# A hybrid attention step: the decode sample as two instruction streams, the sparse keys in a stream of their own, and other margins in the planner's clock

## The chip, the cores and the metric

The kernel runs on one NeuronCore of a Trainium2 chip. The time is the device time of one execution in microseconds (us). Five engines matter: TensorE (PE, with its weight loads counted as PEld), VectorE (DVE), ScalarE (ACT), GpSimd (POOL) and SyncE (SP), which here only issues DMAs. Each works through its own instruction list in the order in which the program wrote it; they wait for each other through semaphores.

## The reference

One layer of an encoder on 2048 prompt frames (16 blocks of 128) and on a decode sample of 8 streams with 16 new frames each (one further block of 128 rows, number 16), which has a cache of 256 rows per stream. RMSNorm, one input projection to 5680 columns, three kinds of attention, a gated output projection with residual, and a final RMSNorm:

```
h = rmsnorm(x) @ w_in          # q, k, v, z of groups A, B, C; indexer iq, iw, ik; forget gate fa
A (8 heads):  causal softmax(q.k*s + c[t]-c[s]) v,  c = cumsum(log_sigmoid(fa + b_f))
B (8 heads, 2 kv heads):  score[t,s] = sum_h iw[t,h]*relu(iq[t,h].ik[s]);  keep the top 256 keys
              softmax(q.k*s + t5_bias[bucket(s-t)]) v  over the kept keys
C (8 heads):  softmax(q.k*s + c_rel[clip(s-t)]) v  over the own chunk of 64 and the 8 before
y = x + concat(oA, oB, oC) * silu(z) @ w_out;  rmsnorm(y)
```

The sample does the same against cache and new rows, with top 68 in B. Keys, values and gates are outputs as well.

## The kernel before, in words

**Arithmetic.** Each float32 operand is split into a high and a low float16 part, and a product is three matmuls. So a projection of 512 tokens by 128 columns is 8 x 3 = 24 matmuls of 512 columns, and each step of attention has a "low" part, Pl, which POOL or DVE subtracts out of the exponentials Pf.

**Streams and the planner.** The program's instructions are not written in a fixed order. Generator functions ("streams") each yield conditions and emit instructions, and `drive` (from line 436) chooses which stream takes its next step. It keeps a model of the engines, `Clock`: `Timed` (line 196 is its call into the engine, which is why the profile puts nearly all instructions on L196) gives each emitted instruction a planned cost, and `Clock.op` a planned end. A stream yields `need(tiles, ps=..., at=...)`, the planned time at which these tiles are ready and the PSUM banks free; or a `gate`, which is 0 or infinite; or `landed`, which waits until a projection group has been stored for 7 us. Conditions without a PSUM bank are "soft": the earliest of them is taken once it is within 200 ns (`AHEAD`) of PE's planned time. Otherwise the first of the other streams, in the order in which they were given, that is ready by PE's planned time takes its step. Streams further behind are so filler. Four services (`exp`, `low`, `evac`, `end`) hold follow-up jobs: exponential, low part, evacuation of a projection, end of a unit. All of this happens when the program is written: on the chip there are only the five lists that come out. PE, ACT, DVE and POOL keep the planned order.

**The work.** First norm and the indexer's projections. Then, in one run of `drive`:

- *Fill*: 21 projection groups, each with 256 weight columns over all 17 blocks (`load_stream`, `fill_stream`, `groups` from line 832). A group is "kv" (key and value columns, stored as outputs) or "qz" (query columns to `qTd`, gates to `szd`). They use the PSUM tag `pj` (two banks). `HO = 'ACCACCAA'` is the order of the eight pairs of dense heads; four qz groups and one kv group of B stand between them. `last[...]` says after which group four heads' projections are complete.
- *Dense units*: 16 heads, A and C in the order of `HO`, four units of 512 queries each (`DenseA`, `DenseC`). A head's keys and values are prepared by `prep_stream` (`K1`, `Ka`, `V` tiles) once its group has landed. The streams `maxima`, `rows`, `scores`, `products` work through the units; four steps of Pf and Pl are in flight (`PB = 4`). Results go to `gTd` (tile `gs`).
- *Indexer and selection*: `score_stream` (tiles `rl`, `acc`) and `select_stream` for blocks 2 to 15. Selection finds the top 256 by a search of ten iterations, in each of which ACT sums signs (`ssg`) and POOL steps the threshold on 128 x 1 tiles (`es`, `eg`, `iv`, `us`, `hv`); then DVE breaks ties, and the mask is stored to `negd`. The last instruction of a block writes `bad` on POOL.
- *Sample* (`sample_stream`, from line 1349): begins when all 14 selections are done, and works in tiles that the indexer and selection no longer use (`acc`, `yy`, `cum`, `eq`, `rl`, `qi`), cut into pieces: keys and query matrix, values, softmax, products. One stream takes the heads in turn: keys in five groups, scores, softmax (`smx`, `smb`), then the products of the head before (`srs`), then this head's values. 16 A and C heads, then its own selection (`select_s`), then 8 B heads. Every four heads are stored to `gTd` (`gs4`, which lies in `yy`).
- *Sparse units* (B, prompt): two per block, in the order 15 down to 0 (`ORDER`). `b_prep` prepares keys, values and biases (`KaB`, `K1B`, `VB`). It stands at the end of `prep_stream`, behind the last dense head's preparation, and waits until the fill has ended, since its tiles take the space of the projection's.
- *Output*: `out_all` opens when all dense units have ended and `b_prep` is through; a block's output projection (72 matmuls of 512 columns from tile `gac`) may begin some time after its sparse units, block 16 when the sample stream is over. It is the last of the fillers.

The streams' order before was: selection, weight loads, products, rows, indexer, scores, maxima, preparation, sample, and as fillers projection and output.

Of the kernel before, what the change touches and what calls it, by code (L numbers as in the profile page):

```python
# [162 lines left out]
class Stream:  # L163


    def __init__(self, steps, slack=SLACK):
        self.steps, self.wait, self.live, self.slack = steps, None, True, slack

    def soft(self):

# [2 lines left out]
    def at(self):  # L173
        if not callable(self.wait):
            return 0.0
        return self.wait() + (0.0 if self.soft() else self.slack)

    def step(self):
        try:
# [5 lines left out]
class Timed:  # L185
# [5 lines left out]
    def __getattr__(self, what):  # L191
# [3 lines left out]
        def call(*args, **kw):  # L195
# [10 lines left out]
            if e == "PE":  # L206
                cost = max(29.0, math.prod(ins[-1].shape[1:]) / 2.4 + 2.5)
                if ins[-1].dtype == F32:
                    cost *= 4
            elif e == "DVE":  # L210
                if what == "scalar_tensor_tensor":
                    cost = (129 if len(ins) > 2 else 68) + 1.042 * m
                elif what == "tensor_copy" and ins[0].dtype != F32:
                    cost = 68 + 0.26 * m if "ps" not in str(ins[0].tensor) else 68 + 0.52 * m
                elif what == "tensor_tensor_scan":
                    cost = 130 + 2.09 * m
                else:
                    cost = 68 + 1.042 * m + (70 if kw.get("accum_out") is not None else 0)
            elif e == "ACT":
                src = (ins or aps)[0]  # L220
                cost = 52 + 0.836 * m + (0 if clock.psum(src) else 40) + (92 if len(ins) > 1 or len(out) > 1 else 0)
                if clock.psum(src) and src.dtype == F16 and "Q" in out[0].tensor.name:
                    cost += 134
            elif e == "POOL":
                if what == "memset":
                    cost = 40 + 0.83 * m
                elif m <= 8:
                    cost = {1: 310, 2: 330, 3: 360}.get(len(ins), 360) if what == "tensor_scalar" else 270
                else:
# [35 lines left out]
def hybrid_step(ctx, tc, x_prompt, x_sample, cache_a_k, cache_a_v, cache_a_logf, cache_b_k, cache_b_v,  # L265
# [150 lines left out]

        return max(clock.slot((ps.key, t), 1 if t in ("tr", "o") else 2) for t in tags)

    def need(*tiles, ps=(), at=0.0):

        return Need(lambda: max(clock.at(*tiles), bank(*ps) if ps else 0.0, at), bool(ps))

    def gate(open_):

# [4 lines left out]
        return lambda: 0.0 if n <= 0 else marks[n - 1] + 7000.0 if len(marks) >= n else INF  # L429

    queues = {k: Queue() for k in ("exp", "low", "evac", "end")}
    services = [Stream(q.steps()) for q in queues.values()]
    for s in services:
        s.step()

# [398 lines left out]
    for k, ch in enumerate(HO):  # L834
        p = npair[ch]
        npair[ch] += 1
        if 2 <= k < 7:
            groups += [(group_b, max(k - 3, 0), int(k > 2))]
            last[2] = last[3] = len(groups)
        if k:  # L840
            groups += [(group_a if ch == "A" else group_c, p, w) for w in range(2)]
        heads += [(ch, 2 * p, len(groups)), (ch, 2 * p + 1, len(groups))]
        last[(0 if ch == "A" else 4) + p // 2] = len(groups)
    loaded, ngr, grouped = [], [0], []

    def load_stream():
# [153 lines left out]
    def scores(i, want_sum, sl, out):  # L1000
# [17 lines left out]
        for k0 in range(0, n, 512):  # L1018
            w = min(512, n - k0)
            for h in range(8):  # L1020
                yield need(qi, kiT, ps=("s1",))
                p = s1()
                mm(p[:, :w], qi[:, h, :], kiT[:, k0:k0 + w], start=True, stop=True)
                r = sl.tile([128, 512], F32, name="rl")
# [321 lines left out]
            G.memset(CN[0:64, 576:640], NEG)  # L1346


    def sample_stream():
        def big(nm, bufs, dt=F16):  # L1350
            return sl.tile([128, SEQ], F32, name=nm, bufs=bufs).bitcast(dt)

# [59 lines left out]
        def load(dst, src, g0, n):  # L1412
            for ap, j0, nj in src:
                a, b = max(j0, g0), min(j0 + nj, g0 + n)
                if a < b:
                    SP.dma_start(dst[:, a - g0:b - g0, :], ap[:, a - j0:b - j0, :])

        def ahead(nm, src):

            def one(g0):  # L1420
                n = min(4, 17 - g0)
                t = row(nm)
                load(t, src, g0, n)
                return t

            nxt = [one(0), one(4)]
            for g0 in range(0, 17, 4):
                yield g0, min(4, 17 - g0), nxt.pop(0)
                if g0 + 8 < 17:
                    nxt.append(one(g0 + 8))  # L1430

        def keys(src):
            Ka = KaS
# [169 lines left out]
            V.tensor_tensor(nsel, wk, acc, ALU.is_equal)  # L1603
            V.tensor_scalar(nsel, nsel, NEG, None, op0=ALU.mult)

        yield from gate_sums()
        yield landed(grouped, last[sorder[0]])
        after = None
        order = [4 * g + r for g in sorder + [2, 3] for r in range(4)] + [0]
        for k, hg in enumerate(order[:-1]):  # L1610
            g, r = divmod(hg, 4)
            if hg == 8:
                if after is not None:
                    yield from after()
                    after = None
                yield from select_s()
                yield landed(grouped, last[2])
            if r == 0:
                qp4 = sl.tile([128, 4, 128], F16, name="qp4", bufs=1)
                q24 = sl.tile([128, 4, 128], F16, name="q24", bufs=1)  # L1620
                rows = [qTd[e, g * 256:(g + 1) * 256, SEQ:NT].rearrange("(h d) t -> d h t", d=64) for e in range(2)]
                SP.dma_start(qp4[0:64], rows[0])
                SP.dma_start(qp4[64:128], rows[0])
                SP.dma_start(q24[0:64], rows[1])
            if hg < 8:
                ks, vs, bias = parts(cak, sak, hg), parts(cav, sav, hg), gate_bias(hg)
            elif hg >= 16:
                ks, vs, bias = parts(cck, sck, hg - 16), parts(ccv, scv, hg - 16), rel_bias(hg - 8)
            else:
                ks, vs, bias = parts(cbk, sbk, g - 2), parts(cbv, sbv, g - 2), rel_bias(hg - 8)  # L1630
            new = hg < 8 or hg >= 16 or r == 0
            more, bias = bias, next(bias)
            if new:
                Ka = yield from keys(ks)
            yield from more
            hl = yield from softmax(qp4[:, r, :], q24[0:64, r, :], Ka, bias)
            if after is not None:
                yield from after()
                yield landed(grouped, last[order[k + 1] // 4])
            if r == 0:  # L1640
                SP.dma_start(sz4, szd[g * 4:(g + 1) * 4, 4, :, 0:64].rearrange("h p d -> p h d"))
            if new:
                yield from values(vs)

            def after(hl=hl, sz=sz4[:, r, :], gs=gs4, r=r, g=g):
                yield from products(*hl, sz, gs[:, r, :])
                if r == 3:
                    for e in range(2):
                        SP.dma_start(gTd[e, g * 256:(g + 1) * 256, SEQ:NT].rearrange("(h d) t -> d h t", d=64),
                                     gs[e * 64:(e + 1) * 64])  # L1650
        yield from after()

    sorder = sorted([0, 1, 4, 5], key=lambda g: last[g])

# [241 lines left out]
    def run(units, may, others, fillers=()):  # L1896
# [41 lines left out]
                queues["end"].add(finished(u))  # L1938
                ndone[0] += 1

        drive(*others[:2], Stream(products()), Stream(rows()), *others[2:3], Stream(scores()), Stream(maxima(), 400.0), *others[3:], *fillers)

    def find_flag():

# [34 lines left out]
    def prep_stream():  # L1979
        for n, h in enumerate(heads):  # L1980
            yield gate(lambda: ndone[0] >= 4 * (n - 1) and (h.kind == "A" or tabled[0]))
            yield landed(grouped, h.after)
            yield from h.prep()
        yield gate(lambda: not fill_s.live)
        yield from b_prep()
        aw_done.append(1)

    aw_done = []

    def smp_stream():  # L1990
        yield gate(lambda: state["selected"] == 14)
        yield from sample_stream()

    def out_all():
        yield gate(lambda: len(ended) >= na and aw_done)
        aw_end.close()
        o = Out()
        closers.append(o.end)

        def open_(b):  # L2000
            if b == 16:
                return not smp_s.live
            n = na + 2 * (ORDER.index(b) + 1)
            return len(ended) >= n and (ended[n - 1] + 12000.0 < clock.t["PE"] or len(ended) == na + len(b_units))

# [2 lines left out]
    for u in units + b_units:  # L2008
        if isinstance(u, DenseA):
            u.open_ = u.head.open_  # L2010
    smp_s = Stream(smp_stream(), 300.0)
    run(units + b_units, lambda u: True, [Stream(select_stream(), 0.0), load_s, Stream(score_stream()), Stream(prep_stream(), 300.0),
                                          smp_s], [fill_s, Stream(out_all())])
    fv = flagged[0]
    closers.pop(1).close()
    sl_end.close()
# [82 lines left out]
```

## Time and profile before

| | |
|---|---|
| median of 3 runs | 2649.38 us (2643.98 to 2650.48) |
| profiled execution | 2649.79 us, span 2648.0 us |
| mean granted PE clock | 0.973 |
| busy share of the span | PE 91%, weight loads 63%, DVE 68%, ACT 52%, POOL 42% |
| instructions | 69046 |
| HBM | 160.37 MB read, 84.85 MB written, 93 GB/s over the span |

How to read it: the page cuts the span into 40 slices (66.2 us each) and gives each engine's busy share in tenths, with the clock that TensorE was granted below. A table by stage does the same for windows that one chooses. A tile's answer lists the instructions that write or read it, with the shortest, median and longest duration in ns and the start of the first and the last. The list of waits says who waited for whom, in us, how often, and the longest. Matmuls overlap: a run of matmuls has a busy time that is shorter than the sum of their durations.

### The profile page before, as it was taken

Reading aid. Unit: us, or ns where it says so; the run is one execution under the profiler, and the core shown is the slowest. Engines: PE = TensorE matmul, PEld = TensorE weight load, DVE = VectorE, ACT = ScalarE, POOL = GpSimd, SP = SyncE. Lnnn points to the kernel's source line nnn. Section 1 sums busy time; section 2 is a strip of 40 time slices with the busy share of each in tenths; the row PEclk is TensorE's granted clock in tenths of the full one; section 3 lists DMA queues with packets and bytes.
Section 4 is the critical chain, followed back from the end, with each engine's and each line's share of the span. In section 5 each row is a group of like instructions: output and inputs, shape, how many; then the busy total and the mean of one; then the engine's idle time right before and its main releaser. Section 6 shows DMA issues by size and latency. Waiting matters only on the chain. (4 is left out here: it accounts for less than half of the span.)

```text
span 2648.0 us, 69046 instructions
## 1 busy us (share of the span) xinstructions
PE 2397.8 (91%) x26752; PEld 1674.7 (63%) x26838; DVE 1802.8 (68%) x4900; ACT 1381.3 (52%) x2734; POOL 1100.3 (42%) x1730
## 2 busy tenths in 40 slices
PE   4998999999999998999999999478899999999995
PEld 3666677766766776686776876355455555555543
DVE  6333778876787868778685566487866677778542
ACT  6324666766656774766744454365554444444110
POOL 0012556663443544534452043255665444544100
PEclk9999999999999999999999999689999999999997
DMA  6247323434343222233445433643533334334531
GB/s 192 60 92 198 92 67 80 107 96 99 94 94 106 71 76 76 72 103 83 120 99 124 120 76 81 135 94 67 144 83 86 79 83 106 84 86 108 127 99 26
DMA packets 553189, 257.24 MB, mean 97 GB/s; under 512 B 376064, under 2 KB 541760, under 8 KB 552592
## 3 DMA queue, kind: packets, MB, share of 16 engines
q1 hardware_dynamic: 552848, 252.71, 38.8%
q8 instruction: 212, 3.47, 0.6%
q14 instruction: 129, 1.06, 0.1%
HBM read 160.37 MB, written 84.85 MB: 93 GB/s over the span
## 5 line engine op out<-in xcount | busy, mean ns | idle before, releaser
L196 POOL TENSOR_TENSOR Pl<-Pf 128x512 f16<-128x512 f32 (+3 forms) x688 | 683.4, 1003 | 582.2 <-ACT Pf L196 544.6
L196 PE MATMUL pj<-wt,hT 128*128 128x128 f16 (+1 forms) x8568 | 779.2, 243 | 11.3 <-DVE ev L196 10.9
L196 PEld LDWEIGHTS <-hT 128*128 128x128 f16 x8976 | 653.2, 98 | 117.5 <-issue 22.0
L196 ACT ACTIVATE Pf<-st,sh 128x512 f32<-128x512 f32 (+1 forms) x496 | 297.9, 613 | 282.9 <-DVE st L196 111.1
L196 PEld LDWEIGHTS <-Pf 128*128 128x128 bf16 x5472 | 314.9, 98 | 104.2 <-issue 9.8
L196 PE MATMUL pj<-wo,gac 128*128 128x512 f16 x1224 | 290.5, 383 | 13.2 <-DMA gac<-gTd 11.6
L196 PE MATMUL pj<-hT,wt 128*128 128x512 f16 (+1 forms) x1440 | 293.6, 348 | 0.3 <-DVE ev L196 0.3
L196 PEld LDWEIGHTS <-Pl 128*128 128x128 f16 x2736 | 255.3, 99 | 18.5 <-POOL Pl L196 16.4
L196 DVE SCALAR_TENSOR_TENSOR acc<-rl,iws,acc 128x512 f32<-128x512 f32 (+3 forms) x266 | 196.2, 738 | 87.1 <-ACT rl L196 82.5
L196 DVE CUSTOM_DVE_ANT_0 jk<-s,ng 128x512 bf16<-128x512 f32 (+3 forms) x304 | 188.7, 621 | 84.6 <-PE s L196 67.4
L196 ACT ACTIVATE Pf<-st,ncb 128x512 f32<-128x512 f32 (+1 forms) x320 | 192.1, 623 | 92.8 <-PE st L196 80.3
L196 DVE TENSOR_REDUCE mx<-s 128x1 f32<-128x512 f32 (+2 forms) x320 | 185.0, 603 | 67.0 <-PE s L196 66.1
L196 ACT ACTIVATE rl<-s 128x512 f32<-128x512 f32 (+3 forms) x304 | 161.3, 544 | 110.8 <-PE s L196 55.7
L196 ACT ACTIVATE ev<-pj 128x512 f32<-128x512 f32 (+4 forms) x211 | 115.2, 546 | 194.0 <-PE pj L196 181.3
L196 PE MATMUL o<-V,Pf 128*128 128x65 f16 x3296 | 213.2, 194 | 1.0 <-ACT Pf L196 0.9
L196 PE MATMUL o<-V,Pl 128*128 128x65 f16 x1648 | 196.2, 193 | 13.3 <-POOL Pl L196 12.3
L196 PEld LDWEIGHTS <-wt 128*128 128x128 f16 x1440 | 126.3, 98 | 129.2 <-issue 13.9
L196 PEld LDWEIGHTS <-gac 128*128 128x128 f16 x1224 | 116.5, 98 | 139.5 <-DMA gac<-gTd 12.7
L196 PE MATMUL st<-qp,Ka 128*128 128x512 f16 (+3 forms) x544 | 180.9, 335 | 8.8 <-ACT Pf L196 8.7
L196 ACT ACTIVATE eq<-acc,us 128x384 bf16<-128x384 f32 (+13 forms) x126 | 165.4, 1313 | 39.6 <-POOL us L196 38.0
L196 PE MATMUL st<-Q,K 98*128 98x512 f16 (+3 forms) x544 | 182.2, 336 | 1.7 <-ACT Q L196 1.7
L196 PE MATMUL o<-VB,Pf 128*128 128x65 f16 (+1 forms) x2176 | 132.4, 194 | 3.6 <-DVE rq_t L196 1.9
(449 smaller groups left out, 4299.8 us busy)
## 6 DMA issues: line engine op xcount, KB each, us to landing
wst<-in_w_in SPq DMA_DIRECT2D x84, 256.0 KB
gac<-gTd SPq DMA_DIRECT2D x34, 384.0 KB
out<-ev SPq DMA_DIRECT2D x96, 128.0 KB
qTd<-ev SPq DMA_DIRECT2D x96, 128.0 KB
szd<-ev SPq DMA_DIRECT2D x96, 128.0 KB
qp<-qTd SPq DMA_DIRECT2D x96, 128.0 KB
out<-xr SPq DMA_DIRECT2D x17, 512.0 KB
xt<-in_x_prompt SPq DMA_DIRECT2D x16, 512.0 KB
```

What stands on the lines that cost most here:

```text
L196: r = f(*args, **kw)
```

## The change

1. The sample becomes two streams. `first` does gate sums, the keys, scores and softmax of each head, and the selection; `second` loads and splits the values and does the products. `first` may be at most two heads' softmaxes ahead (`len(done) >= k - 1`), and each begins the loads of its next head (`begin`) at the end of the one in hand.
2. The streams' order becomes: selection, weight loads, sample first, sample second, products, rows, indexer, scores, maxima, preparation, sparse preparation, and the fillers as before.
3. `b_prep` becomes a stream of its own, gated by the end of the fill alone.
4. The fourth qz group of B moves from before the last two A pairs to the end of the fill; the sample's B heads and the sparse preparation then wait for the whole fill.
5. The planner's clock: a `late` margin for soft conditions (150 ns for the services, 400 for selection, 200 for the indexer), higher planned costs for POOL's `tensor_scalar` on up to 8 columns with two and three operands, and a `room` condition for the indexer's matmul: its output buffer `rl` must be due within 500 ns.

The core of the diff:

```
-        return self.wait() + (0.0 if self.soft() else self.slack)
+        return self.wait() + (self.late if self.soft() else self.slack)
...
-                    cost = {1: 310, 2: 330, 3: 360}.get(len(ins), 360) if what == "tensor_scalar" else 270
+                    cost = {1: 320, 2: 440, 3: 520}.get(len(ins), 520) if what == "tensor_scalar" else 270
...
-    def need(*tiles, ps=(), at=0.0):
-
-        return Need(lambda: max(clock.at(*tiles), bank(*ps) if ps else 0.0, at), bool(ps))
+    def need(*tiles, ps=(), at=0.0, room=None):
+
+        return Need(lambda: max(clock.at(*tiles), bank(*ps) if ps else 0.0, at,
+                                clock.slot((room[0].key, room[1]), room[0].bufs) - 500.0 if room else 0.0), bool(ps))
...
-    services = [Stream(q.steps()) for q in queues.values()]
+    services = [Stream(q.steps(), late=150.0) for q in queues.values()]
...
-        if 2 <= k < 7:
+        if 2 <= k < 6:
             groups += [(group_b, max(k - 3, 0), int(k > 2))]
-            last[2] = last[3] = len(groups)
...
         last[(0 if ch == "A" else 4) + p // 2] = len(groups)
+    groups += [(group_b, 3, 1)]
+    last[2] = last[3] = len(groups)
...
-                yield need(qi, kiT, ps=("s1",))
+                yield need(qi, kiT, ps=("s1",), room=(sl, "rl"))
...
+        def begin(nm, src):
+            early[nm] = [one(nm, src, 0), one(nm, src, 4)]
...
+        def first():
+
+            yield from gate_sums()
+            yield upto(order[0])
+            for k, hg in enumerate(order):
...
+                if fresh(hg):
+                    Ka = yield from keys(stored(hg)[0])
+                yield from more
+                yield gate(lambda: len(done) >= k - 1)
+                weights.append((yield from softmax(qp4[:, r, :], q24[0:64, r, :], Ka, bias)))
+                if k + 1 < len(order):
+                    yield upto(order[k + 1])
+                    if fresh(order[k + 1]) and order[k + 1] != 8:
+                        begin("kn", stored(order[k + 1])[0])
+
+        def second():
+
+            yield upto(order[0])
+            begin("vn", stored(order[0])[1])
+            for k, hg in enumerate(order):
+                g, r = divmod(hg, 4)
+                if fresh(hg):
+                    yield from values(stored(hg)[1])
...
+                if k + 1 < len(order) and fresh(order[k + 1]):
+                    yield upto(order[k + 1])
+                    begin("vn", stored(order[k + 1])[1])
+                yield gate(lambda: len(weights) > k)
+                yield from products(*weights[k], sz4[:, r, :], gs4[:, r, :])
+                done.append(k)
...
-        drive(*others[:2], Stream(products()), Stream(rows()), *others[2:3], Stream(scores()), Stream(maxima(), 400.0), *others[3:], *fillers)
+        drive(*others[:4], Stream(products()), Stream(rows()), *others[4:5], Stream(scores()), Stream(maxima(), 400.0), *others[5:], *fillers)
...
+    def sparse_prep_stream():
         yield gate(lambda: not fill_s.live)
         yield from b_prep()
-        aw_done.append(1)
-
-    aw_done = []
+        prepared.append(1)
...
-        yield gate(lambda: len(ended) >= na and aw_done)
+        yield gate(lambda: len(ended) >= na and len(prepared) == 2)
...
-                return not smp_s.live
+                return not smp2_s.live
...
-    run(units + b_units, lambda u: True, [Stream(select_stream(), 0.0), load_s, Stream(score_stream()), Stream(prep_stream(), 300.0),
-                                          smp_s], [fill_s, Stream(out_all())])
+    smp_s, smp2_s = Stream(smp_stream(), 300.0), Stream(smp2_stream(), 300.0)
+    run(units + b_units, lambda u: True, [Stream(select_stream(), 0.0, 400.0), load_s, smp_s, smp2_s, Stream(score_stream(), late=200.0), Stream(prep_stream(), 300.0),
+                                          Stream(sparse_prep_stream(), 300.0)], [fill_s, Stream(out_all())])
```

More of the change, by code (lines that the diff above doesn't have):

```diff
@@ L163, with __init__ @@
 class Stream:
-    def __init__(self, steps, slack=SLACK):
-        self.steps, self.wait, self.live, self.slack = steps, None, True, slack
+    def __init__(self, steps, slack=SLACK, late=0.0):
+        self.steps, self.wait, self.live, self.slack, self.late = steps, None, True, slack, late
     def soft(self):
@@ L1346, in bias, with sample @@
             G.memset(CN[0:64, 576:640], NEG)
-    def sample_stream():
+    def sample():
         def big(nm, bufs, dt=F16):
@@ L1416, in load, with one @@
                     SP.dma_start(dst[:, a - g0:b - g0, :], ap[:, a - j0:b - j0, :])
-        def ahead(nm, src):
[L1420 to L1426, printed above, removed]
+        def one(nm, src, g0):
+            t = row(nm)
+            load(t, src, g0, min(4, 17 - g0))
+            return t
+        early = {}
+        def ahead(nm, src):
+            nxt = early.pop(nm, None) or [one(nm, src, 0), one(nm, src, 4)]
             for g0 in range(0, 17, 4):
@@ L1429, in ahead @@
                 if g0 + 8 < 17:
-                    nxt.append(one(g0 + 8))
+                    nxt.append(one(nm, src, g0 + 8))
+        def begin(nm, src):
+            early[nm] = [one(nm, src, 0), one(nm, src, 4)]
         def keys(src):
@@ L1604, in select_s @@
             V.tensor_scalar(nsel, nsel, NEG, None, op0=ALU.mult)
[L1606 to L1624, printed above, removed]
-            if hg < 8:
[L1626 to L1646, printed above, removed]
@@ new lines, in stored, with fresh, upto @@
+        def stored(hg):
+            if hg < 8:
+                return parts(cak, sak, hg), parts(cav, sav, hg)
+            if hg >= 16:
+                return parts(cck, sck, hg - 16), parts(ccv, scv, hg - 16)
+            return parts(cbk, sbk, hg // 4 - 2), parts(cbv, sbv, hg // 4 - 2)
+        def fresh(hg):
+            return hg < 8 or hg >= 16 or hg % 4 == 0
+        order = [4 * g + r for g in sorder + [2, 3] for r in range(4)]
+        weights, done = [], []
+        def upto(hg):
+            return landed(grouped, last[hg // 4])
@@ new lines, in first @@
+        def first():
[3 more added lines that the diff above has]
+                g, r = divmod(hg, 4)
+                if hg == 8:
+                    yield gate(lambda: len(done) == k)
+                    yield from select_s()
+                if r == 0:
+                    qp4 = sl.tile([128, 4, 128], F16, name="qp4", bufs=1)
+                    q24 = sl.tile([128, 4, 128], F16, name="q24", bufs=1)
+                    rows = [qTd[e, g * 256:(g + 1) * 256, SEQ:NT].rearrange("(h d) t -> d h t", d=64) for e in range(2)]
+                    SP.dma_start(qp4[0:64], rows[0])
+                    SP.dma_start(qp4[64:128], rows[0])
+                    SP.dma_start(q24[0:64], rows[1])
+                bias = gate_bias(hg) if hg < 8 else rel_bias(hg - 8)
+                more, bias = bias, next(bias)
+                if fresh(hg):
[7 more added lines that the diff above has]
+                        begin("kn", stored(order[k + 1])[0])
@@ new lines, in second @@
+        def second():
+            yield upto(order[0])
+            begin("vn", stored(order[0])[1])
+            for k, hg in enumerate(order):
+                g, r = divmod(hg, 4)
+                if fresh(hg):
+                    yield from values(stored(hg)[1])
+                if r == 0:
+                    SP.dma_start(sz4, szd[g * 4:(g + 1) * 4, 4, :, 0:64].rearrange("h p d -> p h d"))
+                if k + 1 < len(order) and fresh(order[k + 1]):
[4 more added lines that the diff above has]
+                done.append(k)
@@ L1649, in after @@
                         SP.dma_start(gTd[e, g * 256:(g + 1) * 256, SEQ:NT].rearrange("(h d) t -> d h t", d=64),
-                                     gs[e * 64:(e + 1) * 64])
-        yield from after()
+                                     gs4[e * 64:(e + 1) * 64])
+        return first(), second()
     sorder = sorted([0, 1, 4, 5], key=lambda g: last[g])
@@ L1983, in prep_stream, with smp2_stream @@
             yield from h.prep()
+        prepared.append(1)
+    def sparse_prep_stream():
         yield gate(lambda: not fill_s.live)
         yield from b_prep()
-        aw_done.append(1)
-    aw_done = []
+        prepared.append(1)
+    prepared = []
+    halves = []
     def smp_stream():
         yield gate(lambda: state["selected"] == 14)
-        yield from sample_stream()
+        halves.extend(sample())
+        yield from halves[0]
+    def smp2_stream():
+        yield gate(lambda: halves)
+        yield from halves[1]
     def out_all():
-        yield gate(lambda: len(ended) >= na and aw_done)
+        yield gate(lambda: len(ended) >= na and len(prepared) == 2)
         aw_end.close()
@@ L2010, in hybrid_step @@
             u.open_ = u.head.open_
-    smp_s = Stream(smp_stream(), 300.0)
-    run(units + b_units, lambda u: True, [Stream(select_stream(), 0.0), load_s, Stream(score_stream()), Stream(prep_stream(), 300.0),
-                                          smp_s], [fill_s, Stream(out_all())])
+    smp_s, smp2_s = Stream(smp_stream(), 300.0), Stream(smp2_stream(), 300.0)
+    run(units + b_units, lambda u: True, [Stream(select_stream(), 0.0, 400.0), load_s, smp_s, smp2_s, Stream(score_stream(), late=200.0), Stream(prep_stream(), 300.0),
+                                          Stream(sparse_prep_stream(), 300.0)], [fill_s, Stream(out_all())])
     fv = flagged[0]
```

## The prediction

> **What bounds the kernel now.** I read the page first (its time slices), then a table of busy time by stage, then the tiles that mark where a stage begins and ends, then the chain that ended last. The slices show TensorE (PE) nearly full except in three places: the start, slices 27 to 29, and the end.
>
> ```profile
> PE   4998999999999998999999999478899999999995
> PEclk9999999999999999999999999689999999999997
> ```
>
> The table by stage has, after window and length, the busy time of PE, weight loads, VectorE (DVE), ScalarE (ACT) and GpSimd (POOL), then the granted clock, DMA share and GB/s.
>
> ```profile
> 200.00:1600.00 1400.00, 1327.97 (x15456) 1006.16 (x15456) 1016.99 (x2563) 861.79 (x1726) 657.91 (x1251) 0.99 0.39 98
> 1660.00:1740.00 80.00, 42.44 (x452) 28.78 (x448) 40.76 (x109) 31.44 (x75) 17.41 (x22) 0.70 0.59 132
> 1740.00:1860.00 120.00, 99.18 (x1281) 64.23 (x1282) 98.84 (x240) 72.46 (x149) 71.31 (x78) 0.94 0.35 80
> 1860.00:1950.00 90.00, 75.67 (x892) 46.89 (x903) 71.68 (x174) 51.26 (x82) 53.47 (x50) 0.96 0.48 129
> 1950.00:2477.00 527.00, 504.05 (x5276) 300.54 (x5346) 384.52 (x1206) 233.81 (x448) 253.80 (x259) 0.99 0.40 92
> 2477.00:2580.00 103.00, 96.99 (x686) 51.27 (x684) 48.54 (x207) 17.37 (x46) 7.17 (x15) 1.00 0.40 104
> 2580.00:2618.00 38.00, 18.66 (x210) 13.51 (x211) 8.47 (x34) 2.00 (x5) 3.22 (x6) 0.65 0.17 38
> 2618.00:2648.00 30.00, 17.25 (x70) 7.22 (x68) 5.85 (x24) 1.45 (x4) 0.00 (x0) 0.78 0.06 21
> ```
>
> With filler at hand the tensor engine does 1327.97 x 0.99 / 1400 = 0.94 of full-clock work. From 1660 to 1740 it does 42.44 x 0.70 = 29.7 us in 80, from 2580 to 2618 12 us in 38. Tile marks say what these two stretches are:
>
> ```profile
> L196 PE MATMUL pj<-wt,hT x8568: 217/219/421, 48.7 to 1665.8; 128*128 128x128 f16 x114, 128*128 128x256 f16 x86
> L196 DVE COPY K<-Ka x64: 261/281/1016, 245.5 to 1724.3; 64x512 f16<-64x512 f16 x64
> L196 ACT ACTIVATE KaB<-tr x8: 587/597/597, 1749.6 to 1788.6; 128x512 f16<-128x512 f16 x8
> L196 SPq DMA_DIRECT2D gTd<-gs x128: 455/562/1442, 289.6 to 1855.2; - x128
> L196 SPq DMA_DIRECT2D gTd<-gb x32: 366/441/1377, 1928.3 to 2477.9; - x32
> L196 SPq DMA_DIRECT2D gTd<-yy x12: 603/624/894, 1610.8 to 2610.4; - x12
> ```
>
> The filler (projection, first row) ends at 1666. Only then can the last two dense heads have their keys prepared (second row, until 1724); the dense heads before them are out of work, and nothing is left to fill with. That is the hole: dense work waits for the last projection. The sparse keys (third row) are ready at 1789, before the last dense output at 1855, so they hold up nobody. Sparse units end at 2478. The sample's last output is stored at 2610, 132 us after them, and the chain that ended last runs through it:
>
> ```profile
> 2610.37 2.20 DMA gTd<-yy
> 2612.59 5.02 DMA gac<-gTd
> 2617.65 17.61 PE pj L196 x70
> 2635.28 0.70 DVE xr L196
> ```
>
> Sample, store, load, output projection of block 16, norm. So PE work bounds 1950 of the 2648 us, the supply of dense heads bounds the hole, and the sample's serial chain bounds the end. The profiled execution took 2649.8 us with a span of 2648.0, and the median of the runs is 2649.4, so sums against the one hold for the other.
>
> **Part 1, the moved projection group.** The fourth B query/gate group goes from before the last two A pairs to the very end. Its price, from projection rows of 1100 to 1500:
>
> ```profile
> L196 PE MATMUL pj<-wt,hT 128*128 128x128 f16 x1344 | 86.9, 221 | 0.6 <-ACT yy L196 0.4 <-DVE ev L196 0.2
> L196 PE MATMUL pj<-hT,wt 128*128 128x512 f16 x312 | 73.8, 379 | 0.0
> ```
>
> Such a group has 4 x 24 matmuls of 512 columns and 24 + 17 x 24 of 128: 96 x 73.8/312 + 432 x 86.9/1344 = 22.7 + 27.9 = 50.6 us. The last dense pair no longer waits for it, and it remains as filler while that pair is prepared. The hole lost 80 - 29.7 = 50.3 us. Filled at 0.94 it would carry 75.2, so 75.2 - 29.7 = **45 us** come back; the group is just long enough. If the fill runs dry early, as little as 0; at most 50.
>
> [...]
>
> **Part 2, sparse keys in a stream of their own.** They were off the path already (1789 against 1855). Their instructions move with the end of the fill, beside the last dense pair as before. The new gate is the planner's: no engine waits on it. What is issued earlier: 8 key copies of 597 ns on ACT, as many value conversions on ACT and DVE, POOL memsets, and 20 loads on SP's queue; POOL is busy 71.31 of 120 there and ACT 72.46. Zero, between -5 and +5. Without that cover the 39 us from 1750 to 1789 would stand alone.
>
> **Part 3, the sample as two streams.** In the last 171 us these rows share the tensor engine (the sample's are the second to fourth):
>
> ```profile
> L196 PE MATMUL pj<-wo,gac 128*128 128x512 f16 x441 | 100.6, 386 | 12.6 <-DMA gac<-gTd 11.6 <-DVE xr L196 1.0
> L196 PE MATMUL pj<-acc 128*128 128x65 f16 x357 | 14.8, 206 | 8.1 <-DVE acc L196 8.1
> L196 PE MATMUL pj<-yy 128*128 128x256 f16 x48 | 13.6, 316 | 0.9 <-DVE yy L196 0.9
> L196 PE MATMUL pj<-yy,acc 128*128 128x256 f16 x48 | 13.5, 315 | 3.6 <-DVE acc L196 3.6
> ```
>
> A run of such output matmuls at full clock:
>
> ```profile
> 1606.46 2.75 PE L196 MATMUL pj<-hT,wt 128*128 128x512 f16 x12
> ```
>
> (2.75 - 0.38) / 11 = 0.215 us each (0.38 is the last one's own length), so the 441 take 95 us. If the sample has ended by then, the end is 2477 + 95 + 13 (from the last matmul at 2635 to 2648) = 2585: **-63 us**. The sample's work of that window is not gone: PE was busy 96.99 + 18.66 + 17.25 = 132.9, of which 100.6 is output, so 32 us must be done earlier. From 1740 to 1950 PE does 99.18 x 0.94 + 75.67 x 0.96 = 166 us in 210, where 0.94 would be 197: room for 31. VectorE is busy 98.84 of 120 there, so I fill half of it, 16. Net -63 + 32 - 16 = **-47 us** (bounds -63 and -31).
>
> This needs the sample to end in time. It begins when selection ends (1374.6, below) and took until 2610.4: 1236 us. In the code a head's key and softmax side has some 20 planner waits (five key groups with three each, and five), its value and product side some 16 (five groups with two, and six), so two perfect streams take 20/36, 690 us, and two that never overlap 1236. I take 830, nearer to overlap, since the two share only operand tiles and the two projection banks. Filler and output use these banks too, and stand behind the sample in the planner's order; where PE is full that changes who goes first, not the total.
>
> **Part 4, the clock.** The planner emits a step later: 150 ns for the exponential, low-part, evacuation and end jobs, 400 for selection, 200 for the indexer. Selection is one serial chain through ScalarE and GpSimd:
>
> ```profile
> L196 POOL TENSOR_TENSOR bad<-bad,tot x14: 189/190/326, 287.6 to 1374.6; 128x1 f32<-128x1 f32 x14
> ACT eq L196 <- POOL us L196: 38.0, 50, 1.9
> POOL es L196 <- ACT eq L196: 116.6, 107, 3.1
> 1311.56 0.34 POOL L196 TENSOR_SCALAR iv<-eg,hv,iv 128x1 f32<-128x1 f32 x1
> ```
>
> A block has some 52 waits (6 ahead of the ten iterations, 18 in them, some 28 behind). If each loses 400 ns, selection ends 14 x 21 = 290 us later; if other work only slips in where the engine stood idle, 0. I take 150: the sample begins at 1525 and ends at 1525 + 830 = 2355, before the sparse units' 2478 - 45 = 2433. The dearer small POOL operations (8 x 110 + 8 x 160 + 9 x 160 = 3600 ns a block, 50 us in all) turn at most 50 low-part subtractions over to DVE, which has 383 us free between 200 and 1600: zero. The indexer's matmul is now emitted only when its output buffer is due within 500 ns; PE waited for that buffer this long, in order, with dense matmuls behind it:
>
> ```profile
> PE s L196 <- ACT rl L196: 24.2, 34, 3.3
> ```
>
> The 150 ns stand twice in each step's chain, and 688 + 128 of these ran on the two engines:
>
> ```profile
> L196 POOL TENSOR_TENSOR Pl<-Pf x688: 392/1039/3714, 274.4 to 2466.9; 128x512 f16<-128x512 f32 x116, 128x384 f16<-128x384 f32 x27, 128x256 f16<-128x256 f32 x19, 128x128 f16<-128x128 f32 x10
> L196 DVE TENSOR_TENSOR Pl<-Pf x128: 263/679/1524, 288.8 to 2408.7; 128x512 f16<-128x512 f32 x69, 128x256 f16<-128x256 f32 x20, 128x128 f16<-128x128 f32 x20, 128x384 f16<-128x384 f32 x19
> ```
>
> With four steps in flight that is 816 x 0.3 / 4 = 61 us if nothing covers it. Other work covers it outside 1740 to 1950, where about a tenth of the steps lie: **+6 us**. On the other side, PE idles 1400 - 1328 = 72 us between 200 and 1600, these 24 among them; margins and buffers that fit better could win half, -36. So between -36 and +20, a third of the 61.
>
> **Sum:** 2649.8 - 45 - 47 + 6 = 2564 us.
>
> **The rivals.** (a) *The hole moves.* Fill is last in the planner's order; if it starves beside heads 14 and 15, the B group ends late and the sparse keys come after the dense output. For it: from 1740 on PE is not full, yet DVE is near 0.8. Against: 51 us of fill against 190 us of dense work (1666 to 1855). Part 1 is given back: 2564 + 45 = 2609. (b) *The sample is still last, but sooner.* Selection loses the full 290 us and the streams overlap little (three quarters, 927): 1375 + 290 + 927 + 38 (from 2610 to 2648) = 2630. (c) *Slower.* The planner keeps readiness by tile name, and both streams' pieces lie in the same few tiles (keys and values in one tile's halves). If each waits for the other's loads, the pace stays at 1236 us and the start moves by 150: 1375 + 150 + 1236 + 38 = 2799. It decides from the point where delay and duration together pass 1236 us; below about 1140 (an end at 2515, with output left to do) the sample costs nothing. For it: the sample was serial through a stage where PE was half idle, so its own waits set its pace. (d) *No effect:* delay and duration come out near 1236 together, and the hole's gain is hidden behind the same end: 2650.
>
> **How the numbers follow.** Forecast 0.62, (a) 0.13, (b) 0.11, (c) 0.09, (d) 0.05. Less than 0.3% (8 us) cannot be told from no change. Faster: 0.62 + 0.13 + 0.11 = 0.86; same 0.05; slower 0.09. The better bounds of parts 1, 3 and 4 together give 2564 - 5 - 16 - 42 = 2501; all three are unlikely to meet, so the low end takes 44 of these 63: 2520. The high end holds (a) and (b): 2635. Left out are (c), (d) and the forecast's own tails.
>
> **What would show it.** Right: no slice under 8 tenths between 1600 and 1950, and granted clock near 1 there; the last projection matmul after the last dense pair's key copies have begun; the sample's last store before the last sparse one; the ending chain through a prompt block's output. Selection's end shows part 4: 1525 expected, 1665 the bound. Wrong: the last store still the sample's (b, c), a low slice just ahead of the first sparse unit (a), or PE under 0.94 between 200 and 1600 (margins too wide).

## The result, and the profile after

The changed kernel takes 2554.48 us (median of 4 runs, 2544.57 to 2557.49) against 2647.8 before (median of 4 runs; a fourth has moved it from 2649.4). The ratio is 0.9648, with a 95% interval of 0.9628 to 0.9668: 93 us less, where 85 were forecast (2564). The profiled execution took 2557.49 us, its span 2555.6.

The page's slices (63.9 us each) of the changed kernel, TensorE's busy share and its granted clock:

```profile
PE   3998999999999999999999899978799999999997
PEclk7999999999999999999999999998899999999999
```

The deep hole (4, 7, 8) is gone, and the end is full to the last slice. A shallower dip (7, 8, 7, from 1661 to 1853) has stayed in the same place. The same table by stage as before, with the granted clock ahead of the last two numbers (DMA share and GB/s):

```profile
200.00:1600.00 1400.00, 1341.81 (x15807) 1017.60 (x15805) 1063.68 (x2631) 883.50 (x1763) 662.50 (x1255) 0.99 0.39 99
1660.00:1740.00 80.00, 59.57 (x769) 42.53 (x767) 55.95 (x132) 41.06 (x92) 43.69 (x47) 0.88 0.63 143
1740.00:1860.00 120.00, 94.00 (x1037) 57.34 (x1035) 88.58 (x224) 66.87 (x129) 56.66 (x58) 0.87 0.35 91
1860.00:1950.00 90.00, 85.95 (x1011) 53.54 (x1010) 67.20 (x198) 47.87 (x92) 48.31 (x50) 1.00 0.44 106
1950.00:2477.00 527.00, 512.76 (x5431) 305.38 (x5429) 379.82 (x1228) 218.43 (x422) 239.86 (x252) 1.00 0.40 94
2477.00:2555.60 78.60, 65.78 (x305) 29.66 (x303) 28.57 (x119) 6.52 (x18) 0.00 (x0) 0.94 0.30 86
```

From 1660 to 1740 PE now carries 59.57 x 0.88 = 52 us of full-clock work instead of 30, from 1740 to 1860 only 94.00 x 0.87 = 82 instead of 93. Between 200 and 1600 it is busy 1342 us instead of 1328, a gain that the forecast had only as a bound. The stage marks, in the order of before (last projection, last dense key copies, sparse keys, last dense, sparse and sample stores), and the last instruction of selection:

```profile
L196 PE MATMUL pj<-wt,hT x8568: 217/219/421, 48.7 to 1670.7; 128*128 128x128 f16 x112, 128*128 128x256 f16 x88
L196 DVE COPY K<-Ka x64: 252/278/817, 246.6 to 1633.4; 64x512 f16<-64x512 f16 x64
L196 ACT ACTIVATE KaB<-tr x8: 589/598/620, 1706.6 to 1768.6; 128x512 f16<-128x512 f16 x8
L196 SPq DMA_DIRECT2D gTd<-gs x128: 455/542/1726, 288.9 to 1804.9; - x128
L196 SPq DMA_DIRECT2D gTd<-gb x32: 364/488/1262, 1885.4 to 2468.1; - x32
L196 SPq DMA_DIRECT2D gTd<-yy x12: 597/610/648, 1594.3 to 2361.5; - x12
L196 POOL TENSOR_TENSOR bad<-bad,tot x14: 191/191/245, 295.1 to 1408.6; 128x1 f32<-128x1 f32 x14
```

The projection still ends at 1671 (1666 before), but the last dense pair no longer waits for its end: its key copies are done at 1633 instead of 1724, and dense work at 1805 instead of 1855. The sample ends at 2361, 107 us ahead of the sparse units, where it had ended 132 us behind them. The last long pieces of the chain that ended last (start, length, what):

```profile
2456.94 3.88 PE pj L196 x18
2461.19 81.60 PE pj L196 x378
```

378 output matmuls in a row in 81.60 us, 0.216 each: a prompt block's output is now last, and TensorE sets the end.

### The profile page after: what moved, and what is told of

It is laid out like the page before. It is cut to its first block, busy times and chain, and to the rows that moved or that the text cites. A ratio compares the mean times of both kernels' runs of the same rounds, so it can differ in the third digit from the quotient of the medians.

```text
span 2555.6 us, 69095 instructions
## 1 busy us (share of the span) xinstructions
PE 2377.3 (93%) x26838; PEld 1666.3 (65%) x26838; DVE 1821.7 (71%) x4921; ACT 1378.0 (54%) x2734; POOL 1082.6 (42%) x1709
## 4 chain that ended last, share of the span: by engine, by line
PE 64%; DVE 16%; DMA 7%; issue 5%; ACT 4%; POOL 4%; SPq 1%; DVEq 0%; ACTq 0%; POOLq 0%
PE pj L196 41%; PE st L196 9%; PE o L196 6%; PE s L196 6%; DVE jk L196 2%; DVE acc L196 2%; DVE mx L196 2%; POOL Pl L196 1%; PE tr L196 1%; DMA wst<-in_w_in 1%; ACT eq L196 1%; ACT Pf L196 1%; DMA qp<-qTd 1%; DVE wt L196 1%; SPq L196 1%
## 5 line engine op out<-in xcount | busy, mean ns | idle before, releaser
L196 POOL TENSOR_TENSOR Pl<-Pf 128x512 f16<-128x512 f32 (+3 forms) x667 | 660.6, 1002 | 584.5 <-ACT Pf L196 557.7
L196 PE MATMUL pj<-wo,gac 128*128 128x512 f16 x1224 | 284.8, 379 | 0.0
L196 DVE CUSTOM_DVE_ANT_0 jk<-s,ng 128x512 bf16<-128x512 f32 (+3 forms) x304 | 188.6, 620 | 79.8 <-PE s L196 63.9
L196 DVE CUSTOM_DVE_ANT_0 jk<-s,CN 128x512 bf16<-128x512 f32 (+1 forms) x224 | 108.6, 485 | 34.6 <-PE s L196 24.9
```

The lines of the kernel that those rows point to most:

```text
L196: r = f(*args, **kw)
```

## The experiments

Times are medians against the kernel before on the same chip (2646.7 to 2648.3 in each set of runs), with the 95% interval of the ratio. Rows quoted are those of the last stores, as above. First each part alone, put into the kernel before.

**The moved group alone.**

```
-        if 2 <= k < 7:
+        if 2 <= k < 6:
...
+    groups += [(group_b, 3, 1)]
+    last[2] = last[3] = len(groups)
```

> The kernel before with only the fourth B query/gate group moved to the end of the fill. Theory A (the terms of the forecast add up): the hole of 1660 to 1740 fills, -45 us, 2603. Theory B (as long as the sample is one stream, its chain sets the end, whatever is gained ahead of it): last dense store some 45 us earlier, but the sample's last store stays near 2610 and the time within 15 us of before, 2635 to 2650.

2659.37 against 2646.73, ratio 1.003 (1.0016 to 1.0045): slower, by 8 us as the ratio has it and 13 as the medians have it.

```profile
L196 SPq DMA_DIRECT2D gTd<-gs x128: 455/562/1103, 288.1 to 1801.7; - x128
L196 SPq DMA_DIRECT2D gTd<-gb x32: 360/472/927, 1882.5 to 2416.0; - x32
L196 SPq DMA_DIRECT2D gTd<-yy x12: 603/615/647, 1646.7 to 2622.6; - x12
```

Dense work ends 54 us earlier and the sparse units 62 us earlier, as the forecast's first part has it. None of it reaches the end, because the sample's last store has moved from 2610 to 2623 and still sets it. That is theory B's case.

**The two streams alone.** The diff's `sample()` with `first` and `second` and its place in the order; old clock, old groups.

> The kernel before with only the sample as two streams (at the head of the planner's order, old clock, old group order). Theory A: -47 us, 2602, with the hole still there. Theory B: the same -47 or more (to -60), the sample's last store well before the last sparse store. If the streams wait for each other through shared tiles (rival c): no gain, last store at 2610 or later.

2617.06, ratio 0.9874 (0.9847 to 0.9900): 33 us faster.

```profile
L196 SPq DMA_DIRECT2D gTd<-gs x128: 456/564/1785, 286.3 to 1888.3; - x128
L196 SPq DMA_DIRECT2D gTd<-gb x32: 360/490/1334, 1955.2 to 2536.5; - x32
L196 SPq DMA_DIRECT2D gTd<-yy x12: 605/612/1252, 1524.2 to 2224.3; - x12
```

The sample ends at 2224, 386 us earlier, so rival (c), streams that hold each other up, is out. But dense work ends 33 us later than before (1888) and the sparse units 59 us later (2537): sample work that had stood at the idle end now takes its place ahead of them. The gain is less than the 47 that both theories expected. This sample needs 2224.3 - 1368.9 = 855 us from the end of selection, near the 830 of the forecast.

**The clock alone.** All of `late`, the dearer POOL costs and `room`, nothing else.

> The kernel before with only the planner's clock changed (margins, dearer small POOL operations, room for the indexer's buffer). Theory A: +6 us, between -36 and +20. Theory C (the margins let PE do more between 200 and 1400, where it was busy 21 us longer in the changed kernel): PE busy there near 1154 instead of 1134; in the total 0 while the sample's chain sets the end, or -20 if selection ends as early as before and the sample with it.

2640.93, ratio 0.9978 (0.9962 to 0.9994): 6 us faster, hardly more than can be told from nothing.

```profile
L196 SPq DMA_DIRECT2D gTd<-gs x128: 451/522/1222, 286.1 to 1802.2; - x128
L196 SPq DMA_DIRECT2D gTd<-gb x32: 359/487/904, 1870.5 to 2408.8; - x32
L196 SPq DMA_DIRECT2D gTd<-yy x12: 605/610/653, 1655.3 to 2601.2; - x12
```

The sparse units end 69 us earlier than before, more than by any other part alone, and the sample's store at 2601 hides it. By stage:

```profile
200.00:1400.00 1200.00, 1150.48 (x13357) 872.80 (x13357) 930.09 (x2310) 773.18 (x1521) 581.29 (x1155) 1.00 0.38 98
```

Before, the same 1200 us held 12998 matmuls in 1133.53 us of busy time. This is theory C's case: the planner's figures alone bring 17 us of PE work forward.

**The sparse preparation alone.** `sparse_prep_stream` split off, nothing else.

> The kernel before with only the sparse preparation in a stream of its own. Both theories: no change, within 5 us, since the sparse keys were ready 66 us before the last dense output; the key copies may begin before the last dense pair's are done.

2655.53, ratio 1.003 (1.0015 to 1.0044): slower by 8 us, where at most 5 was expected.

```profile
L196 DVE COPY K<-Ka x64: 259/281/1015, 246.1 to 1738.8; 64x512 f16<-64x512 f16 x64
L196 ACT ACTIVATE KaB<-tr x8: 578/596/597, 1701.6 to 1738.4; 128x512 f16<-128x512 f16 x8
L196 SPq DMA_DIRECT2D gTd<-yy x12: 602/630/1657, 1610.0 to 2621.1; - x12
```

The sparse keys are now prepared beside the last dense pair's (both until 1739), which are so done 15 us later than before (1724); dense work ends at 1859 (1855 before). The sample's last store slips by 11 us: between its stores at 1825 and 2107 it takes 282 us, where the kernel before took 260. That the preparations take each other's time fits the rows; what slows the sample there was not tried. Each edit makes the planner lay out the whole program anew, and this one moved the time by 8 us with no step of the forecast behind it, so a difference of a few us in the other runs is weak evidence on the part that was edited.

The four alone add up to some 23 us less. Together they bring 93. So the next runs take one part at a time out of the changed kernel.

**Back to one sample stream.** The old `sample_stream` at its old place, all else as changed.

> The changed kernel with the sample back in one stream, at its old place in the order; group, clock and sparse preparation as changed. Theory B (a one-stream sample sets the end whatever is gained ahead of it, as in the runs with the group or the clock alone): last sparse store at 2410 or earlier, the sample's last store near 2600 to 2620, time 2635 to 2655. Theory A (terms add up): 2554 + 47 = 2601.

2643.72, ratio 0.9985 (0.9969 to 1.0002).

```profile
L196 SPq DMA_DIRECT2D gTd<-gb x32: 366/496/1908, 1846.4 to 2376.3; - x32
L196 SPq DMA_DIRECT2D gTd<-yy x12: 606/614/651, 1663.2 to 2601.9; - x12
```

This settles between A and B. The sparse units end at 2376, 102 us earlier than before, and the time is not to be told from the kernel before: the one-stream sample ends at 2602 whatever stands ahead of it. In the changed kernel the two streams, with their place in the order, are worth 89 us.

**Back to the old clock.**

```
-    services = [Stream(q.steps(), late=150.0) for q in queues.values()]
+    services = [Stream(q.steps()) for q in queues.values()]
...
-                    cost = {1: 320, 2: 440, 3: 520}.get(len(ins), 520) if what == "tensor_scalar" else 270
+                    cost = {1: 310, 2: 330, 3: 360}.get(len(ins), 360) if what == "tensor_scalar" else 270
```

(and the other margins and `room`)

> The changed kernel with the old clock. Theory A: 2554 - 6 = 2548. Theory C (the margins are worth the PE work that the clock alone brought ahead by 1400, some 30 us of it): 2580 to 2590, PE busy between 200 and 1400 back at 1134.

2607.08, ratio 0.9842 (0.9809 to 0.9875): the clock is worth 53 us, more than theory C's 30 and against theory A, which had it cost 6.

```profile
200.00:1400.00 1200.00, 1135.52 (x13004) 858.81 (x13002) 898.85 (x2248) 760.27 (x1505) 590.83 (x1172) 0.99 0.38 96
```

PE is busy 1136 us again between 200 and 1400. In the changed kernel:

```profile
200.00:1400.00 1200.00, 1154.22 (x13347) 879.55 (x13345) 932.06 (x2317) 777.28 (x1531) 577.50 (x1153) 0.99 0.38 99
```

**Back to the old group order.**

> The changed kernel with the old group order. Theory A: 2554 + 45 = 2599. Theory C (the clock alone already ended the dense work at 1802, as early as the whole change did at 1805, so group and clock fill the same hole): 2560 to 2575.

2599.59, ratio 0.9815 (0.9782 to 0.9849): the moved group is worth 45 us, as theory A has it. Theory C was wrong here. The clock alone ended dense work at 1802, but only while the sample was one slow stream; with two streams and the old order it ends at 1848:

```profile
L196 SPq DMA_DIRECT2D gTd<-gs x128: 455/520/1645, 284.7 to 1848.2; - x128
```

**Two groups at the end.** An attempt at the dip that is left.

```
-        if 2 <= k < 6:
+        if 2 <= k < 5:
...
-    groups += [(group_b, 3, 1)]
+    groups += [(group_b, 2, 1), (group_b, 3, 1)]
```

> The changed kernel with two B query/gate groups at the end of the fill instead of one. It lost most where no filler is left, 1680 to 1885 (PE 162 of 205 busy at 0.88). If the supply of dense heads is still what opens it: last dense store 40 to 50 us earlier, the stretch shorter, 2525 to 2545. If the sparse keys (ready some 100 us after the fill) become the wait: a new hole ahead of the first sparse unit, 2550 or more.

2577.82, ratio 0.9736 (0.9703 to 0.9770): 23 us slower than with one.

```profile
PE   3998999999999999999999999994789999999998
```
```profile
L196 PE MATMUL pj<-wt,hT x8568: 216/219/421, 48.6 to 1735.5; 128*128 128x128 f16 x115, 128*128 128x256 f16 x85
L196 ACT ACTIVATE KaB<-tr x8: 588/593/598, 1764.8 to 1788.2; 128x512 f16<-128x512 f16 x8
L196 SPq DMA_DIRECT2D gTd<-gs x128: 455/540/1616, 285.3 to 1726.0; - x128
```

Dense work ends at 1726, 79 us earlier, but the fill ends at 1736, 65 us later, and the sparse keys wait for it until 1788. The hole is back (4), now between dense and sparse: this edit brings about rival (a).

**What in the clock?** Three runs take one of its parts out of the changed kernel: all margins at 0, the old POOL costs, no `room`.

> The changed kernel with all late margins at 0 (services, selection, indexer); dearer POOL operations and room kept. The clock as a whole was worth 53 us (2607 with the old one). Theory M (the margins carry it): 2590 to 2607, and matmuls between 200 and 1400 back from 13347 toward 13004. Theory N (costs or room carry it): 2550 to 2565.

> The changed kernel with the old planned costs of small POOL operations. Theory M: 2550 to 2565. Theory N: 2590 or more; ScalarE's wait for the threshold, 38 us before and 19 in the changed kernel, back near 38.

> The changed kernel without the room condition for the indexer's buffer. PE's wait for that buffer (11 us between 200 and 1400, 24 before) back near 24, and at most those 13 us in the time: 2554 to 2567.

Without margins 2557.99 (ratio 0.9671, 0.9649 to 0.9694), without room 2558.44 (0.9668, 0.9652 to 0.9684): neither is apart from the changed kernel (0.9648, 0.9628 to 0.9668). With the old costs 2583.05 (0.9762, 0.9746 to 0.9779): 29 us slower than the changed kernel. The margins do not carry the clock's gain by themselves, so theory M is out; theory N had put the old costs at 2590 or more, and they fall 7 us short of it. About half of the 29 us shows before 1400, where PE is busy 14 us less than in the changed kernel:

```profile
200.00:1400.00 1200.00, 1140.51 (x13117) 866.81 (x13115) 911.36 (x2253) 767.58 (x1510) 598.35 (x1175) 0.99 0.38 96
```

The low-part rows with the old costs, and then of the changed kernel:

```profile
L196 POOL TENSOR_TENSOR Pl<-Pf x696: 389/1039/6259, 270.4 to 2473.5; 128x512 f16<-128x512 f32 x119, 128x128 f16<-128x128 f32 x20, 128x256 f16<-128x256 f32 x19, 128x384 f16<-128x384 f32 x16
L196 DVE TENSOR_TENSOR Pl<-Pf x120: 279/680/1554, 307.1 to 2462.8; 128x512 f16<-128x512 f32 x67, 128x128 f16<-128x128 f32 x21, 128x256 f16<-128x256 f32 x16, 128x384 f16<-128x384 f32 x16
```
```profile
L196 POOL TENSOR_TENSOR Pl<-Pf x667: 394/1041/3907, 273.9 to 2459.4; 128x512 f16<-128x512 f32 x116, 128x128 f16<-128x128 f32 x20, 128x256 f16<-128x256 f32 x17, 128x384 f16<-128x384 f32 x14
L196 DVE TENSOR_TENSOR Pl<-Pf x149: 276/680/1480, 278.0 to 2405.5; 128x512 f16<-128x512 f32 x79, 128x384 f16<-128x384 f32 x25, 128x256 f16<-128x256 f32 x23, 128x128 f16<-128x128 f32 x22
```

With the dearer costs the planner hands 29 more subtractions to VectorE (149 for 120), and the longest on POOL falls from 6.3 to 3.9 us. That the fall of the longest pays is not shown, since without `room`, and as fast as the changed kernel, it is 5.8 us:

```profile
L196 POOL TENSOR_TENSOR Pl<-Pf x677: 390/1041/5810, 275.0 to 2460.1; 128x512 f16<-128x512 f32 x118, 128x256 f16<-128x256 f32 x18, 128x128 f16<-128x128 f32 x17, 128x384 f16<-128x384 f32 x17
```

ScalarE's wait for the threshold is not what pays either. It is 19 us in the changed kernel and came back in both runs, with the old costs and without margins, and only the first was slower. In this order:

```profile
ACT eq L196 <- POOL us L196: 19.4, 27, 1.7
```
```profile
ACT eq L196 <- POOL us L196: 34.3, 45, 2.0
```
```profile
ACT eq L196 <- POOL us L196: 36.7, 46, 2.0
```

Whether it is the 29 moved subtractions, or the later planned thresholds that go with them, was not tried apart: the costs are worth 29 us, and how they come by it stays open. Without room, PE's wait for the indexer's buffer stayed low (9.4 us in all, 11.0 in the changed kernel and 24.8 with the old clock), against what was expected, so something else in the clock had lowered it. The three parts make 29 + 4 + 4 = 36 of the clock's 53 us one by one, and the two fours are within the noise; the rest shows only when they go together.

Without margins selection's last instruction is at 1363.7 instead of 1408.6 (the row `bad<-bad,tot` of that run): the margins delay selection by 45 us, and the time does not show it.

**The sample behind in the order.**

```
-        drive(*others[:4], Stream(products()), Stream(rows()), *others[4:5], Stream(scores()), Stream(maxima(), 400.0), *others[5:], *fillers)
+        drive(*others[:1], *others[1:2], Stream(products()), Stream(rows()), *others[4:5], Stream(scores()), Stream(maxima(), 400.0), *others[5:], *others[2:4], *fillers)
```

> The changed kernel with both sample streams behind the sparse preparation in the planner's order, just ahead of the fillers. The forecast's claim (where PE is full the order changes who goes first, not the total; the sample had 107 us to spare): 2545 to 2565, the sample's last store later than 2361 but before the last sparse one. Against it: its pace is set by its place in the order, it ends last again and the time passes 2600.

2540.22, ratio 0.9593 (0.9574 to 0.9613): 14 us faster than the change, the fastest version here.

```profile
L196 SPq DMA_DIRECT2D gTd<-gb x32: 359/489/1097, 1871.4 to 2408.9; - x32
L196 SPq DMA_DIRECT2D gTd<-yy x12: 594/629/2152, 1596.8 to 2455.8; - x12
```

The sparse units end 59 us earlier than in the changed kernel (2409 for 2468), the sample 94 us later (2456). It ends after the sparse units, against what was expected, but while output blocks are left to do, so it delays nothing. The chain that ended last runs through those blocks here too:

```profile
2401.44 130.18 PE pj L196 x816
```

The claim that order does not change the total is off by 14 us here, which is not far above the 8 us of the sparse preparation. This run also parts the split from its place: it differs from the run with one sample stream only in the split, for in both the sample stands just ahead of the fillers. 2540 against 2644, so the split alone is worth some 104 us in this setting, and the place at the head of the order gains nothing.

## Why the prediction was right, and where it was not

The time came out 9.5 us under the forecast, well inside its range and with its mechanism: no hole where the dense heads waited, and no sample at the end. Step by step:

- **What bounds the kernel.** Right. That the sample's chain set the end is shown most plainly by the kernel with everything but the two streams: sparse work 102 us earlier, time unchanged. (The low slices of the kernel before are 26 to 29, one earlier than the prediction counts them.)
- **Part 1, -45.** Right in size: taking the group back costs 45 us. But it holds only with the sample split; alone it is worth nothing. The sign that was named for it, no slice under 8 tenths and a clock near 1, did not appear: the dip of 7, 8, 7 lies from 1661 to 1853, at a mean clock of 0.88 and 0.87. The last projection matmul starts at 1671, so from there on dense work has no filler left.
- **Part 2, 0.** Alone 8 us slower, outside the bounds of 5. Inside the whole change it was not taken out, so what it does there is not known.
- **Part 3, -47.** The condition held: the sample needed 2361.5 - 1408.6 = 953 us from selection's end, not 830, but began at 1409 and not at 1525, and ended at 2361 against 2355 forecast. That the end came within 6 us is luck, since the two errors cancel. With the streams alone it needed 855 us, and 1048 behind in the order, so its pace also depends on what stands beside it. The term was mis-sized: 33 alone, 89 in the whole change. It had been priced as if what the other parts win ahead of the sample counted without it. The sparse units were expected to end at 2433 and ended at 2468. The two streams at the head of the order take their time from them: with the sample behind they end at 2409, with one stream at 2376.
- **Part 4, +6.** Wrong in sign and size: -53 in the whole change, outside the bounds of -36 and +20 (alone -6). The step that failed is the sentence that the dearer small POOL operations cost zero; putting the old costs back costs 29 us. The estimate looked at whether VectorE had room for what moves over (it had, and 29 operations moved where at most 50 were allowed for) and not at what a plan nearer to the chip is worth. That the nearness pays is argued and not shown, but the new costs are nearer: from the start of such an operation to the start of the next, where that one follows without a wait, the kernel before took 0.48 us with two operands and 0.63 and 0.56 with three (means of `eg`, `iv` and `us`; 0.47, 0.67 and 0.48 in the changed kernel), where the planner had counted 0.33 and 0.36 and now counts 0.44 and 0.52. Selection was put 150 us later and was 34 (1408.6 for 1374.6).

That 85 and 93 lie so close is in part luck: parts 3 and 4 were both too small, and the sum counted three terms that are not independent. Taken out one by one they are worth 45, 89 and 53, together 187; put in one by one -8, 33 and 6, together 31. The two sums bracket the 93.

None of the rivals came about. Against (a), the sparse keys are ready at 1769, before the last dense store at 1805. Against (b), (c) and (d), delay and duration came to 34 + 953 = 987 us, under the 1140 from which the sample costs.

The row's 0.70 is a mean of two values. The clock records in the traces of the two kernels show no others than 1 and 0.5: in the hole before, 48 of the 80 us from 1660 to 1740 were at half clock, and in the dip of the changed kernel 51 of the 205 us from 1680 to 1885. The means 0.70 and 0.88 are mixtures of the two. By that record, PE's 42.44 busy us in the hole carried 30.7 us of full-clock work, 1 us from the 29.7 of the prediction's sum.

## What to carry to other kernels

When a serial side job ends last, whatever is won ahead of it is invisible: first split or shorten that job, and only then judge other changes, or each of them will look worthless alone. Read such a gain from the marks of each stage (here the last dense and sparse stores), not from the time. Where a program is laid out by a model of the engines, correct the model's cost for the smallest operations too: the planned costs of the small POOL operations alone moved this kernel by 29 us.

## What the hardware showed that was not expected

The same threshold instruction on POOL, 128 x 1, took 0.34 us in one layout and 0.56 in another (median). These are its rows (shortest, median and longest in ns) before and in the changed kernel:

```profile
L196 POOL TENSOR_SCALAR us<-es,iv,us x112: 334/558/1477, 245.2 to 1316.2; 128x1 f32<-128x1 f32 x112
```
```profile
L196 POOL TENSOR_SCALAR us<-es,iv,us x112: 337/344/1786, 248.8 to 1348.6; 128x1 f32<-128x1 f32 x112
```

On POOL its predecessor is the same in both (`iv` 98 times, `es` 14 times). One thing that differs between the two traces is its company on VectorE. Where no SCALAR_TENSOR_TENSOR of VectorE runs during its first 0.34 us, its median is 0.34 us in both kernels (60 of the 112 before, 68 of 112 after); where one does, it is 0.78 and 0.69 (52 and 44). In the kernel before 61 of the 112 took more than 0.4 us, 42 of them in this company; in the changed kernel 44, of them 29. So the slow ones mostly have this company, and fewer of them leave the median at 0.34. That is what falls together in time, counted in these two traces and not tried by an edit, and it does not hold for all: 19 and 15 of those without this company took more than 0.4 us. It is also not what the planned costs are worth: with the old costs put back its median is 0.34 as well, and that kernel is 29 us slower.

The clock records of the same two traces, set beside PE's busy time in them, also show what went ahead of a change of TensorE's clock in these two executions. The stretches at half clock inside the program are multiples of 3.41 us, up to 27.3 us before and 20.5 in the changed kernel. The program is cut here into windows of that length, with the record's changes on their edges, from 260 us on to 60 us before the end. The changed kernel's clock falls to half 12 times, after windows in which PE is busy at most 0.44 of the time, and stays full after all of 0.50 and more; in the kernel before, it falls 16 times, after windows of up to 0.51, and stays full after some from 0.47 on. The returns come after busier windows: in the changed kernel windows of up to 0.84 leave it at half, and it returns after windows that are full; in the kernel before, it stays at half after windows of up to 0.80 and returns from 0.92 on. In the dip of the changed kernel PE is busy 162 of 205 us, about four fifths, and its clock falls eight times all the same, after windows in which PE was busy 0.06 to 0.44: the idle time lies bunched there.
